# Query and key projections of one attention layer, from three 256-column products to one of 256 and one of 512 in two PSUM banks

## The chip, the cores and the metric

The kernel runs on one core of one Trainium2 chip. The metric is the device time of one execution in microseconds (us), and the figure that is compared is the median of several runs.

## The reference

An encoder of four layers on 256 tokens with 1024 features in float32. Each layer has a half-step SwiGLU block, a token mixer and a second half-step SwiGLU block, every one behind an RMSNorm and added to the residual. The mixer of the first layer, the one that the change touches, is attention in three groups (windows of 128, 512 and 2048 with dilations 1, 4 and 16), eight heads of 64 in each, mixed by a softmax over the groups' log-sum-exps:

```python
qkv = (u @ w_qkv).reshape(b, s, N_GROUPS_A, 3, HEADS_PER_GROUP, HEAD_DIM_A)
for g, (win, dil) in enumerate(DIL_PATTERNS):
    o, l = _dilated_group(qkv[:, :, g, 0], qkv[:, :, g, 1], qkv[:, :, g, 2], win, dil, ...)
wts = jax.nn.softmax(jnp.stack(lses, 0), axis=0)
o = jnp.einsum('gbsh,gbshd->bshd', wts, jnp.stack(outs, 0))
return o.reshape(b, s, ATTN_WIDTH).astype(u.dtype) @ w_o
```

## The kernel before

**High and low parts.** Every large product is made of float32 operands that are split into a high part (fp32r, rounded) and a low part (the rest): w = wh + wl, x = xh + xl, and w·x is taken as wh·xh + wh·xl + wl·xh. `mm3` issues these (through `mm`, L91; transposes are L94) as three matmuls of 256 columns into the same 256 columns of a PSUM bank. `wide`, which the SwiGLU blocks use, issues two: wl·xh with 256 columns, and wh with both parts of x side by side in 512 columns. The two halves of a bank then hold wl·xh + wh·xh and wh·xl, and are added when the bank is read.

**Weights.** They come in blocks of 128x2048. `dma_block` (L169) loads one on SP's queue into one of four `raw` buffers. `split_block` makes the high part on ScalarE (`w`, L178) and the low part on VectorE (`w`, L181) in one of four `w` buffers. `take` hands a block to the products in a fixed order, `done` counts one as used up, and `pump(n)` splits as many new blocks as were used up, n at most. All engines' instructions are issued in the order of the program; there is no scheduler.

**PSUM.** There are eight banks, four called A and four called B. In this stage `ab()` gives the B bank that was taken longest ago, and `dbank(j)` gives A bank j. Taking a bank waits for nothing by itself: its first matmul waits until the last readers of the bank's earlier contents are done.

**The attention stage (`mix0`).** `vproj` makes the values of the three groups. `proj(hp, g)` makes queries and keys of head pair hp in group g (hp from 0 to 3, g from 0 to 2): eight steps k over the 1024 input features, each of them for c = 0 (queries, 128 features) and c = 1 (keys). The eighth step reads the bank on VectorE, times the norm factors `Rqk` (L1068), into `qk`. The twelve projections are called p00 to p32 here, by hp and g.

The other pieces are `S(i)` for head pair i // 2 and query half i % 2 (scores of two heads: matmuls A<-qk, then `s` L1097 and the row maximum `m` L1100 on VectorE), `E(u)` (exponential, ScalarE, L1107), `N(u)` (division by the sum, VectorE, L1115), `T(u)` (four transposes on TensorE, L94, and a copy to `pt` on ScalarE, L1125) and `V(hp)` (products of `pt` and `vt`, into a bank of `ab()`, read by ScalarE and VectorE into `og`, L656 and L657). `S` and `T` use A banks for the first three head pairs, and banks of `ab()` for the last.

p00, p01 and p02 stand alone. Then, for hp = 0, 1, 2, the pieces of head pair hp are interleaved with the 24 steps of the projections of hp + 1:

```python
def part(i, a, b, c, pump=0, lead=0):
    u = 2 * i
    r = [(None, lead), (lambda: S(i), 0)]
    if i and i % 2 == 0:
        r.append((lambda: V(i // 2 - 1), 0))
    r += [(lambda f=f, n=n: f(u + n), 0) for f in (E, N) for n in range(2)]
    return r + [(lambda: self.pump(pump), a), (lambda: T(u), b), (lambda: T(u + 1), c)]
```

The number beside each piece says how many steps follow it: `lead` steps ahead of S, 6 after the pump, 2 after the first T, 4 (less the lead) after the second. For the last head pair there is no projection left. S(6) stands right behind p32, and its filler is the output projection (`A<-og,w`).

Of the kernel before, what the change touches and what calls it, by code (L numbers as in the profile page):

```python
# [11 lines left out]
AF = mybir.ActivationFunctionType  # L12
ALU = mybir.AluOpType
# [25 lines left out]
class Enc:  # L39
# [973 lines left out]
    def mix0(self):  # L1013
        nc = self.nc
# [32 lines left out]
        Rqk = self.sb(ev, [128, 512], F32, "Rqk")  # L1047
# [6 lines left out]
        def proj(hp, g):  # L1054

            def step(k, state={}):
                if k == 0:
                    state["w"] = self.take(("qk", hp, g))
                    state["p"] = self.ab()
                w, p = state["w"], state["p"]  # L1060
                for c in range(2):
                    sl = slice(128 * c, 128 * c + 128)
                    self.mm3(p[:, 256 * c:256 * c + 256], w[:, :, k, sl], self.xk(k),
                             start=k == 0 and c == 0, stop=k == 7)
                if k == 7:
                    self.done()
                    q = self.sb(ev, [128, 512], F32, f"qk{g}", 2)
                    nc.vector.tensor_tensor(q, p, Rqk, ALU.mult)  # L1068
                    qk[hp, g] = q
                    if hp == 0 and g < 2:  # L1070
                        self.pump()
            st = {}
            return [lambda k=k: step(k, st) for k in range(8)]
# [83 lines left out]
        def pfill(hp):  # L1157
            return [f for g in range(3) for f in proj(hp, g)]
# [8 lines that stand above are left out]
            return r + [(lambda: self.pump(pump), a), (lambda: T(u), b), (lambda: T(u + 1), c)]  # L1167

        for hp in range(3):
            lead = 2 if hp else 0  # L1170
            self.interleave(part(2 * hp, 6, 2, 4 - lead, 2, lead) + part(2 * hp + 1, 6, 2, 4, 1), pfill(hp + 1))

        r = [lambda f=f, u=u: f(u) for f, u in
# [492 lines left out]
```

## Time and profile before

| | |
|---|---|
| median of 3 runs | 1922.9 us (1922.87 to 1923.37) |
| profiled execution, its own time | 1922.22 us |
| its span, first to last instruction | 1920.4 us |
| TensorE busy | 1895.0 us (99%) |
| VectorE busy | 1401.6 us (73%) |
| ScalarE busy | 999.2 us (52%) |
| mean granted TensorE clock | 0.997 |

The span is the part of an execution that the trace covers, and 1.8 us of the execution's time lie around it. PE is TensorE's matmuls, PEld its weight loads, DVE VectorE, ACT ScalarE, SP the queue of the loads. Matmul ends are modelled, so the time of one matmul in a row is read from starts: the next start less this one.

### The profile page before, as it was taken

The page shows a single profiled execution, that of the slowest core. Times are in us where ns is not written, and L with a number is a line of the kernel's source. Part 1 is how long each engine was busy: PE and PEld are TensorE (multiplying, and loading weights), DVE is VectorE, ACT ScalarE, POOL GpSimd, SP SyncE. Part 2 cuts the span into 40 slices and gives each one's busy share as a digit, 9 for nine tenths or more (in the row PEclk, how much of TensorE's full clock was granted, in tenths as well). Part 3 has the DMA queues.
Part 4 walks back from the last instruction along what each step waited for, and adds up shares of the span by engine and source line. Part 5 has one row for each costly group of instructions (what it writes and reads, how often), then busy time and mean ns, then how long its engine had stood idle before and what let it go on. Part 6 is the DMA issues. An engine that isn't in the chain of part 4 may idle for free.

```text
span 1920.4 us, 28519 instructions
## 1 busy us (share of the span) xinstructions
PE 1895.0 (99%) x11936; PEld 1662.2 (87%) x11936; DVE 1401.6 (73%) x1877; ACT 999.2 (52%) x1272; POOL 10.7 (1%) x28
## 2 busy tenths in 40 slices
PE   8999999999999999999999999999999999999998
PEld 7888899888888898788888889988888888788887
DVE  7776667876687787887768776787777766678774
ACT  6554444655464544655446454555445546746543
POOL 0000000000000000000000000000000000000000
PEclk9999999999999999999999999999999999999999
DMA  7655533465555544256546554365546544435650
GB/s 266 222 195 192 192 132 132 154 219 190 183 187 194 194 162 147 89 179 216 179 172 208 187 184 168 132 219 192 181 162 223 203 162 159 154 111 183 212 184 36
DMA packets 48689, 338.63 MB, mean 176 GB/s; under 512 B 5488, under 2 KB 5664, under 8 KB 8240
## 3 DMA queue, kind: packets, MB, share of 16 engines
q1 hardware_dynamic: 47952, 335.11, 50.1%
q8 instruction: 93, 1.52, 0.3%
q0 software_dynamic: 608, 1.71, 0.3%
q14 instruction: 36, 0.29, 0.0%
HBM read 335.74 MB, written 1.05 MB: 175 GB/s over the span
## 4 chain that ended last, share of the span: by engine, by line
PE 90%; DVE 5%; ACT 2%; issue 1%; DMA 0%; SPq 0%; DVEq 0%; POOL 0%; POOLq 0%; ACTq 0%
PE B L91 47%; PE A L91 42%; DVE w L181 1%; ACT w L178 1%; DVE zc L787 1%; PE A L94 0%; DMA h<-in_x_dram 0%; DVE x L315 0%; ACT x L313 0%; DVE h L292 0%; DVE acc L366 0%; PE B L94 0%; DVE h L290 0%; SPq L225 0%; DVE s L1097 0%
## 5 line engine op out<-in xcount | busy, mean ns | idle before, releaser
L181 DVE TENSOR_TENSOR w<-raw,w 128x2048 fp32r<-128x2048 f32 x315 | 719.3, 2290 | 274.4 <-ACT w L178 274.3
L178 ACT ACTIVATE w<-raw 128x2048 fp32r<-128x2048 f32 x315 | 598.5, 1909 | 99.9 <-PE B L91 40.7
L91 PE MATMUL B<-x,w 128*128 128x256 f32 (+1 forms) x3968 | 641.5, 321 | 2.7 <-DVE w L181 1.5
L91 PEld LDWEIGHTS B<-x,w 128*128 128x128 f32 x3968 | 569.5, 189 | 69.8 <-issue 2.7
L91 PE MATMUL A<-x,w 128*128 128x256 f32 x3008 | 521.6, 335 | 9.7 <-DVE w L657 7.5
L91 PEld LDWEIGHTS A<-x,w 128*128 128x128 f32 x3008 | 455.6, 189 | 72.9 <-DVE w L657 7.5
L91 PE MATMUL B<-g,w 128*128 128x256 f32 (+1 forms) x1408 | 250.8, 336 | 0.0
L91 PE MATMUL A<-g,w 128*128 128x256 f32 (+1 forms) x1408 | 250.4, 336 | 0.0
L91 PEld LDWEIGHTS A<-g,w 128*128 128x128 f32 x1408 | 216.7, 187 | 31.4
L91 PEld LDWEIGHTS B<-g,w 128*128 128x128 f32 x1408 | 216.6, 187 | 31.4
L656 ACT ACTIVATE g<-br 128x512 fp32r<-128x512 f32 x88 | 55.6, 632 | 250.1 <-DVE br L497 250.1
L491 DVE TENSOR_TENSOR sl<-sl,R 128x512 f32<-128x512 f32 x176 | 120.3, 687 | 2.5
L657 DVE TENSOR_TENSOR g<-br,g 128x512 fp32r<-128x512 f32 x88 | 60.9, 692 | 61.5 <-ACT g L656 61.5
L313 ACT ACTIVATE x<-h,cols 128x256 fp32r<-128x256 f32 x88 | 39.9, 501 | 70.9 <-DVE h L290 51.2
L483 ACT ACTIVATE br<-A 128x256 f32<-128x256 f32 x88 | 30.4, 386 | 74.9 <-PE A L91 74.9
L483 ACT ACTIVATE br<-B 128x256 f32<-128x256 f32 x88 | 30.3, 385 | 74.8 <-PE B L91 74.8
L494 ACT ACTIVATE sl<-sl 128x512 f32<-128x512 f32 x88 | 55.0, 628 | 25.8 <-DVE sl L491 25.8
L497 DVE TENSOR_TENSOR br<-sl,br 128x512 f32<-128x512 f32 x88 | 60.4, 686 | 0.6
L483 ACT ACTIVATE sl<-A 128x256 f32<-128x256 f32 x88 | 30.1, 378 | 52.0 <-PE A L91 52.0
L483 ACT ACTIVATE sl<-B 128x256 f32<-128x256 f32 x88 | 29.8, 377 | 49.5 <-PE B L91 49.5
L91 PE MATMUL B<-w,x 128*128 128x512 f32 (+1 forms) x216 | 50.0, 379 | 0.0
L488 DVE TENSOR_TENSOR sl<-sl,A 128x256 f32<-128x256 f32 x88 | 33.1, 416 | 21.8 <-ACT sl L483 21.8
(290 smaller groups left out, 1085.6 us busy)
## 6 DMA issues: line engine op xcount, KB each, us to landing
raw<-in_ffn_w_dram SPq DMA_DIRECT2D x262, 1024.0 KB, 4.8
raw<-in_attn_w_qk_dram SPq DMA_DIRECT2D x12, 1024.0 KB, 4.8
raw<-in_conv_w_pw_dram SPq DMA_DIRECT2D x12, 1024.0 KB, 4.8
raw<-in_gla_w_vr_dram SPq DMA_DIRECT2D x8, 1024.0 KB, 5.5
raw<-in_attn_w_v_dram SPq DMA_DIRECT2D x6, 1024.0 KB, 4.7
raw<-in_fnet_w_dram SPq DMA_DIRECT2D x4, 1024.0 KB, 4.8
raw<-in_gla_w_in_dram SPq DMA_DIRECT2D x4, 1024.0 KB, 4.8
raw<-in_gla_w_o_dram SPq DMA_DIRECT2D x4, 1024.0 KB, 4.7
```

What stands on the lines that cost most here:

```text
L91: return self.nc.tensor.matmul(out, lhsT, rhs, start=start, stop=stop, skip_group_check=True)
L178: self.nc.scalar.activation(w[:, 0], raw, AF.Copy)
L181: (eng or self.nc.vector).tensor_tensor(w[:, 1], raw, f32(w[:, 0]), ALU.subtract)
L313: nc.scalar.activation(xh[:, c], h[:, c], AF.Copy, scale=g[c])
L483: nc.scalar.activation(t[:, c], P[c][:, 1], AF.Copy)
L488: nc.vector.tensor_tensor(t[:, c], t[:, c], P[c][:, 0], ALU.add)
L491: nc.vector.tensor_tensor(t, t, self.Rb(), ALU.mult)
L494: nc.scalar.activation(t, t, AF.Silu)
L497: nc.vector.tensor_tensor(br, sl, br, ALU.mult)
L656: self.nc.scalar.activation(p[:, 0], src, AF.Copy)
L657: self.nc.vector.tensor_tensor(p[:, 1], src, f32(p[:, 0]), ALU.subtract)
L787: nc.vector.scalar_tensor_tensor(o, x, w, o, ALU.mult, ALU.add)
```

## The change

In `proj` each step issues, for each c, the two matmuls of `wide` in place of the three of `mm3`, and queries and keys have a bank each, so a projection takes two banks of `ab()` where it took one. After the eighth step ScalarE copies the upper half of each bank to `q` (two copies), VectorE adds the lower half of each (two additions), and then multiplies by `Rqk`. For hp = 1 and 2 the lead is three steps where it was two, and the steps after the second T are one where they were two.

```diff
             def step(k, state={}):
                 if k == 0:
                     state["w"] = self.take(("qk", hp, g))
-                    state["p"] = self.ab()
+                    state["p"] = [self.v2(self.ab()) for _ in range(2)]
                 w, p = state["w"], state["p"]
                 for c in range(2):
-                    sl = slice(128 * c, 128 * c + 128)
-                    self.mm3(p[:, 256 * c:256 * c + 256], w[:, :, k, sl], self.xk(k),
-                             start=k == 0 and c == 0, stop=k == 7)
+                    self.wide(p, c, w[:, :, :, 128 * c:128 * c + 128], k, self.xk(k), k == 0, k == 7)
                 if k == 7:
                     self.done()
                     q = self.sb(ev, [128, 512], F32, f"qk{g}", 2)
-                    nc.vector.tensor_tensor(q, p, Rqk, ALU.mult)
+                    for c in range(2):
+                        nc.scalar.activation(q[:, 256 * c:256 * c + 256], p[c][:, 1], AF.Copy)
+                    for c in range(2):
+                        o = q[:, 256 * c:256 * c + 256]
+                        nc.vector.tensor_tensor(o, o, p[c][:, 0], ALU.add)
+                    nc.vector.tensor_tensor(q, q, Rqk, ALU.mult)
                     qk[hp, g] = q
...
         for hp in range(3):
-            lead = 2 if hp else 0
+            lead = 3 if hp else 0
             self.interleave(part(2 * hp, 6, 2, 4 - lead, 2, lead) + part(2 * hp + 1, 6, 2, 4, 1), pfill(hp + 1))
```

`wide`, which it now calls:

```python
def wide(self, p, c, w, k, x, start, stop):
    self.mm(p[c][:, 0], w[:, 1, k], x[:, 0], start, False)
    self.mm(p[c], w[:, 0, k], x, False, stop)
```

## Rows read from the trace of the kernel before

**Rows 1.** Page, part 1: busy time of each engine over the span.
```profile
PE 1895.0 (99%) x11936; PEld 1662.2 (87%) x11936; DVE 1401.6 (73%) x1877; ACT 999.2 (52%) x1272; POOL 10.7 (1%) x28
```

**Rows 2.** Busy time by stretch (engines, clock, DMA share, GB/s): projections, interleaved part, SwiGLU.
```profile
229.60:246.80 17.20, 17.20 (x145) 17.14 (x143) 8.26 (x5) 7.72 (x6) 0.00 (x0) 1.00 0.58 190
246.80:315.40 68.60, 68.60 (x602) 65.74 (x600) 49.21 (x91) 31.25 (x46) 0.00 (x0) 1.00 0.34 123
...
370.00:470.00 100.00, 100.00 (x577) 87.37 (x576) 74.49 (x80) 54.92 (x66) 0.00 (x0) 1.00 0.61 210
```

**Rows 3.** TensorE in order of time, attention stage: start, us, line, operands, count.
```profile
229.51 17.43 PE L91 MATMUL B<-x,w 128*128 128x256 f32 x144
246.88 1.35 PE L91 MATMUL A<-qk 64*128 64x256 f32 x12
248.15 4.58 PE L91 MATMUL B<-x,w 128*128 128x256 f32 x36
...
270.04 1.15 PE L91 MATMUL A<-qk 64*128 64x256 f32 x12
271.12 1.96 PE L91 MATMUL B<-pt,vt 128*64 128x256 f32 x24
273.01 4.58 PE L91 MATMUL B<-x,w 128*128 128x256 f32 x36
277.43 0.60 PE L94 MATMUL A<-ident,e 128*128 128x128 f32 x4
...
296.43 4.58 PE L91 MATMUL B<-x,w 128*128 128x256 f32 x36
...
315.44 2.23 PE L91 MATMUL B<-qk 64*128 64x256 f32 x24
317.78 1.96 PE L91 MATMUL B<-pt,vt 128*64 128x256 f32 x24
```

**Rows 4.** ScalarE in order of time, after S(2) and V(0).
```profile
275.02 3.70 ACT L178 ACTIVATE w<-raw 128x2048 fp32r<-128x2048 f32 x2
```

**Rows 5.** VectorE in order of time, p02, p11, p20 and p30 being read.
```profile
246.99 0.69 DVE L1068 TENSOR_TENSOR qk<-B,Rqk 128x512 f32<-128x512 f32 x1 [1.52 <-PE B L91]
...
266.90 0.68 DVE L1068 TENSOR_TENSOR qk<-B,Rqk 128x512 f32<-128x512 f32 x1
...
276.95 4.49 DVE L181 TENSOR_TENSOR w<-raw,w 128x2048 fp32r<-128x2048 f32 x2 [1.12 <-ACT w L178]
281.36 0.69 DVE L1068 TENSOR_TENSOR qk<-B,Rqk 128x512 f32<-128x512 f32 x1
...
304.78 0.68 DVE L1068 TENSOR_TENSOR qk<-B,Rqk 128x512 f32<-128x512 f32 x1
```

**Rows 6.** Order of time in a SwiGLU block: copies and additions of halves.
```profile
383.45 0.63 ACT L483 ACTIVATE sl<-B 128x256 f32<-128x256 f32 x2
...
386.19 0.74 DVE L488 TENSOR_TENSOR sl<-sl,B 128x256 f32<-128x256 f32 x2
```

**Rows 7.** What TensorE waited for, whole span: total us, times, longest.
```profile
PE A L91 <- DVE w L657: 7.5, 1, 7.5
PE B L91 <- DVE lr L406: 1.7, 1, 1.7
```

**Rows 8.** Busy time by stretch around a fall of the granted clock.
```profile
780.00:785.00 5.00, 3.87 (x32) 3.35 (x24) 4.40 (x9) 4.17 (x8) 0.00 (x0) 1.00 0.01 2
785.00:788.00 3.00, 1.29 (x6) 1.04 (x6) 2.63 (x9) 1.86 (x4) 0.00 (x0) 0.70 0.00 0
788.00:790.00 2.00, 0.85 (x4) 0.73 (x4) 0.59 (x3) 1.20 (x2) 0.00 (x0) 0.50 0.00 0
790.00:792.00 2.00, 2.00 (x12) 2.00 (x10) 0.70 (x3) 1.20 (x2) 0.00 (x0) 0.50 0.00 0
792.00:794.00 2.00, 2.00 (x14) 2.00 (x14) 1.70 (x5) 1.26 (x3) 0.00 (x0) 0.74 0.00 0
...
800.00:802.00 2.00, 2.00 (x19) 2.00 (x18) 2.00 (x2) 2.00 (x5) 0.00 (x0) 1.00 0.72 295
```

## Prediction

> **What bounds the kernel now.** I read the page's busy times first: TensorE is busy for 99% of the span, VectorE for 73%, ScalarE for 52% [rows 1]. That is an average over twelve stages, so the windows of the attention stage come next. While the first three projections run, and while the others are interleaved with scores and transposes, TensorE is busy without a gap, VectorE for 49.2 of 68.6 us and ScalarE for 31.3 [rows 2]. So here TensorE sets the end: each nanosecond that its own instructions lose or gain moves the end, and so does each wait that is put in front of it. The other engines' work is free as long as TensorE finds what it needs. So I looked for what TensorE will need under the change that it does not need now, and read the three engines in order of time around the two places where a projection ends just before other work depends on it.
>
> **Products.** Before, p00 to p02 run alone: 144 matmuls from 229.51 to 246.88 [rows 3], 17.37 us, 120.6 ns for each, so 724 ns for a step of six. The form after runs in the SwiGLU blocks: 577 matmuls in 100 us, half of 256 and half of 512 columns, with the same shapes of weights and x [rows 2], so 347 ns for a pair and 694 ns for a step of two pairs. The columns of a step are the same, 1536. If columns alone counted, the gain would be nothing, the lower bound. The weight loads tell the forms apart: in the projections PEld is busy for 17.14 of 17.20 us, in the SwiGLU stretch for 87.4 of 100 [rows 2], so the old form also stands at the pace of its loads, one of which the new form drops. I take the pitches as they are: 29.5 ns a step, 96 steps, **-2.8 us**.
>
> The Trainium skill (TensorE: Matmul & The Clock Gate, Back-to-back issue gap) puts an isolated matmul at its columns over 2.4 GHz and about 2.5 ns. By it 192 matmuls fewer would give 0.5 us, an estimate from that page; the rows show some 14 ns more than the columns for each matmul in both forms, and the measurement decides.
>
> **More reading of banks.** For each projection ScalarE gets two copies (0.63 us a pair) and VectorE two additions (0.74 us a pair) [rows 6]; the multiplication stays. Over twelve that is 7.6 and 8.9 us. VectorE has 19 us idle in the interleaved part alone, ScalarE 37 [rows 2], so neither becomes the bound by its sum. The order of their queues is another matter.
>
> **Scores right behind a projection.** S(0) follows p02 and S(6) follows p32 with nothing between. The first two groups of their products need older projections, the third needs the newest. Before, VectorE's multiplication starts 0.11 us after TensorE reaches S(0) and takes 0.69 [rows 3, 5]. S(0) takes 1.27 us, S(6) and S(7) together 2.34, where S(2), with steps ahead of it, takes 1.08 [rows 3], so the chain just shows. After, the chain is longer by the copies (0.63), the second addition (0.42, the first lies beside the second copy) and a hand-over of some 0.05: 1.1 us, all visible, since it showed already. Both engines are idle then. Two places: **+2.2 us**. The lower bound is 0, if other work lay between; none does. At S(2) and S(4) three steps (2.1 us) and the first two groups cover a chain of 1.9 us: nothing.
>
> **Banks.** This is the part that decides. `ab()` hands out the four B banks in a ring. Call the ring's places 0 to 3. A projection now takes two, V one. With hp = 0 there is no V, and the projections alternate between pairs: p10 has 0, 1; p11 has 2, 3; p12 has 0, 1. Then p20 takes 2, 3 at its first step, V(0) takes 0, and p21 gets 1 and 2. So p21's second bank, for its keys, is the one that holds p20's queries, and p20 has only just ended. p22 gets 3, 0; p30 gets 1, 2; V(1) gets 3; p31 gets 0 and 1, and 1 again holds the queries of the projection that has just ended. Twice, then, the third matmul of a projection (its first for c = 1) has to wait until VectorE has added the first half of the projection before. With one bank a projection, p20, V(0) and p21 had 0, 1 and 2, and nothing met.
>
> How late is that addition? p20's last step lies behind V(0), five steps on. The six steps after the pump are k = 3 to 7 of p20 and k = 0 of p21. TensorE leaves V(0) at 273.01 [rows 3]; five steps and one pair later, 3.47 + 0.35 = 3.82 us, it stands before the wait. But the pump ahead of these steps has put two blocks on ScalarE (275.02, 3.70 us) and VectorE (276.95, 4.49 us) [rows 4, 5]. In the trace p20's multiplication starts at 281.36, though TensorE had ended p20 by 277.43 [rows 3, 5]; no one was waiting for it. That is 8.35 us after V(0), and for p30 it is 304.78 - 296.43, again 8.35 [rows 3, 5]. That chain (scores, maximum, exponential, splits) does not hang on the steps, so it stays where it is relative to V. p20's copies queue behind the same splits on ScalarE, which end at 278.72 [rows 4], and are done well before. So the first addition takes the place of the multiplication: 8.35 + 0.42 + 0.05 = 8.82 us after V(0). The wait is 8.82 - 3.82 = 5.0 us. TensorE's matmuls stand in one queue, so T(4), T(5), the steps and S(3) all wait behind it, and no other engine catches this up. Two places: **+10.0 us**. The upper bound is a wait for all of p20's reading, the second addition and the multiplication too: 1.0 us more at each, 12. The lower bound is 0, if the additions could go ahead of the splits; the queue's order excludes it, unless I have the ring wrong. All other banks come free in time: the nearest is p20's, whose earlier content is p11. Its multiplication starts at 266.90 [rows 5], so two additions in that place end at 267.64; p12 ends two steps ahead of S(2) at 270.04 [rows 3], 268.59, less 0.35 for its twelve shorter steps: p20 starts 0.6 us after the additions.
>
> **The clock.** After the first 8 us the longest wait of TensorE in this trace is 1.7 us [rows 7]. Around it the granted clock fell to its lower level, 1.2 GHz: 0.70 in one stretch, 0.50 in two, 0.74 in the next [rows 8], which makes 1.8 + 4.0 + 1.0 = 6.8 us at that level. Before the fall TensorE had been busy for 3.87 of 5 us, then for 1.29 of 3, partly with thin products. A wait of 5.0 us inside dense work has no like in the trace. I take it that the clock falls at each. In the low stretch TensorE started 12 matmuls in 2 us against 19 at 2.4 GHz [rows 8], so each microsecond loses 0.37. Between no fall and 6.8 us of work at the lower level lie 0 and 2.5 us for each wait. Part of a low stretch passes during the wait, so I take half: **+2.6 us** for both, bounds 0 and 5.0.
>
> The Trainium skill (TensorE: Matmul & The Clock Gate, A second HAM failure mode: psum-queue depth-cycling) tells of a kernel that went in turn through PSUM banks and whose clock swung between both levels because TensorE idled between groups of matmuls. It speaks against this change; rows 8 agree that gaps can bring the clock down, but show no gap over a bank.
>
> **The sum.** -2.8 + 2.2 + 10.0 + 2.6 = +12.0 us against the profiled execution's own 1922.2 us: 1934.2. The median of the runs stands 0.7 us above that execution, so 1934.9, and I forecast **1935 us**.
>
> **Rivals.**
> 1. No wait for the banks, because I have the ring or the reader wrong: -2.8 + 2.2, 1922.3 us, no change. It decides if VectorE's first addition is done 3.8 us after V. For it speaks that a bank is waited for only where readers overlap; against it stands that the multiplication at 281.36 is late by far more than a step.
> 2. One of the two places stays free, say because a piece falls on another place of the ring: 1922.9 - 0.6 + 5.0 + 1.3 = 1928.6 us. The equal 8.35 us at both speak against it.
> 3. VectorE also comes too late for S(2) and S(4). Its slack there is about 1.0 us. A block split 2.29 us long in its way would cost 1.3 us at each, 1937.5 us. In the trace VectorE waits for TensorE ahead of p02 [rows 5], and nothing is pumped between p11 and S(2), which speaks against it.
>
> **How the numbers follow.** Both waits as worked out, with or without the clock: 0.84. Rival 1: 0.08, rival 2: 0.04, rival 3: 0.04. The forecast is the first. Its bounds, from the median: without the clock 1922.9 + 9.4 = 1932.3; with 12 us of waits and 5.0 of clock 1939.3. No gain from the products would add 2.8. The range is **1929 to 1939 us**: from about rival 2 to the upper bound, with rival 1 and some of the rest left out. A measurement of this kernel can tell 0.2% from no change, 3.8 us, so slower is anything over 1926.7. Slower gets all but rival 1 and a little: 0.90. Rival 1 gives 0.08 to no change, and 0.02 to faster, should the scores' chain be hidden too.
>
> **What would show it.** In the changed kernel's order of time TensorE stands still for about 5 us twice, one pair into p21 and into p31, released by an addition of VectorE into `qk` that starts right behind two splits. The granted clock is low for some microseconds behind each. S(0) takes about 2.4 us, S(6) with S(7) about 3.4. Steps in the projections take 694 ns. I am wrong if TensorE runs through p21 without a gap, if the gap is much shorter because VectorE gets to the addition before the splits, or if the clock stays at its full level throughout.

## The result, and the profile after

The changed kernel takes 1935.74 us (median of 4 runs, 1935.08 to 1936.74) against 1922.88 us for the kernel before (4 runs, 1920.91 to 1923.37), a ratio of 1.0071 with a 95% interval from 1.0059 to 1.0082: 12.9 us slower, outside the 0.2% that tell a change from none. The forecast was 1935 us in 1929 to 1939. The profiled execution took 1936.74 us, the slowest of its four; its span is 1935.0 us.

The page's first part after the change, beside [rows 1]: 192 matmuls fewer, 24 instructions more each on VectorE and ScalarE. TensorE is busy for 3.8 us more, with fewer matmuls, and idle for 36.2 us of the span where it was 25.4; where that lies, the page does not say.

```profile
PE 1898.8 (98%) x11744; PEld 1655.3 (86%) x11744; DVE 1411.1 (73%) x1901; ACT 1007.1 (52%) x1296; POOL 10.7 (1%) x28
```

What TensorE waited for in the attention stage (total us, times, longest). Before, the only such wait from 200 to 340 us was one of 0.2 us. L1070 is the addition of the halves, L1071 the multiplication by `Rqk`.

```profile
PE B L91 <- DVE qk L1070: 9.4, 2, 4.7
PE A L91 <- DVE qk L1071: 0.8, 1, 0.8
PE B L91 <- DVE qk L1071: 0.8, 1, 0.8
PE B L94 <- DVE e L1118: 0.3, 1, 0.3
```

TensorE in order of time, which answers to [rows 3]:

```profile
230.26 17.11 PE L91 MATMUL B<-x,w 128*128 128x256 f32 x96
247.30 0.92 PE L91 MATMUL A<-qk 64*128 64x256 f32 x8
249.03 0.49 PE L91 MATMUL A<-qk 64*128 64x128 f32 x4 [0.80 <-DVE qk L1071]
249.45 4.45 PE L91 MATMUL B<-x,w 128*128 128x256 f32 x24
...
272.60 1.96 PE L91 MATMUL B<-pt,vt 128*64 128x256 f32 x24
274.49 4.15 PE L91 MATMUL B<-x,w 128*128 128x256 f32 x22
283.31 1.01 PE L91 MATMUL B<-x,w 128*128 128x256 f32 x2 [4.68 <-DVE qk L1070]
...
288.98 1.15 PE L91 MATMUL A<-qk 64*128 64x256 f32 x12
...
302.69 1.96 PE L91 MATMUL B<-pt,vt 128*64 128x256 f32 x24
304.58 4.15 PE L91 MATMUL B<-x,w 128*128 128x256 f32 x22
313.41 1.01 PE L91 MATMUL B<-x,w 128*128 128x256 f32 x2 [4.68 <-DVE qk L1070]
...
319.36 1.15 PE L91 MATMUL A<-qk 64*128 64x256 f32 x12
...
329.85 0.92 PE L91 MATMUL B<-qk 64*128 64x256 f32 x8
331.57 1.37 PE L91 MATMUL B<-qk 64*128 64x128 f32 x16 [0.80 <-DVE qk L1071]
332.97 1.96 PE L91 MATMUL B<-pt,vt 128*64 128x256 f32 x24
```

The 22 matmuls behind V(0) are k = 3 to 7 of p20 and the pair for c = 0 of p21. The first matmul for c = 1 starts 8.82 us after V(0) has ended (283.31 - 274.49), and 8.83 after V(1).

VectorE around the end of p02 and of p20 and p30, beside [rows 5]:

```profile
247.48 0.77 DVE L1070 TENSOR_TENSOR qk<-qk,B 128x256 f32<-128x256 f32 x2 [1.20 <-ACT qk L1067]
248.28 0.69 DVE L1071 TENSOR_TENSOR qk<-qk,Rqk 128x512 f32<-128x512 f32 x1
...
278.43 4.49 DVE L181 TENSOR_TENSOR w<-raw,w 128x2048 fp32r<-128x2048 f32 x2 [1.13 <-ACT w L178]
282.85 0.74 DVE L1070 TENSOR_TENSOR qk<-qk,B 128x256 f32<-128x256 f32 x2
...
312.94 0.75 DVE L1070 TENSOR_TENSOR qk<-qk,B 128x256 f32<-128x256 f32 x2
```

The additions start where the two subtractions end. 282.85 and 0.42 for the first make 283.27, and TensorE starts at 283.31. ScalarE is no part of it: p20's copies start at 280.10.

The granted clock (the figure behind POOL's) around the two waits, in windows, beside [rows 8]:

```profile
281.00:284.00 3.00, 0.69 (x2) 0.63 (x3) 2.97 (x4) 0.00 (x0) 0.00 (x0) 0.52 0.72 240
284.00:288.00 4.00, 4.00 (x16) 3.41 (x15) 0.31 (x1) 0.60 (x1) 0.00 (x0) 0.51 0.88 340
288.00:292.00 4.00, 4.00 (x30) 3.32 (x29) 1.81 (x6) 0.81 (x2) 0.00 (x0) 1.00 0.01 4
...
312.00:314.00 2.00, 0.59 (x2) 0.59 (x3) 1.97 (x4) 0.00 (x0) 0.00 (x0) 0.50 0.82 311
314.00:318.00 4.00, 4.00 (x15) 3.35 (x15) 0.41 (x1) 0.60 (x1) 0.00 (x0) 0.50 0.84 352
318.00:320.00 2.00, 2.00 (x14) 1.67 (x14) 0.00 (x0) 0.60 (x1) 0.00 (x0) 0.83 0.00 0
```

The clock falls to 1.2 GHz while TensorE stands still. By these windows it is low for 6.8 us at each place, and 4.6 and 5.3 us of that lie behind the wait: 15 or 16 matmuls start in 4 us, then 30.

### The profile page after: what moved, and what is told of

It reads as the page before. It is cut to its first block, busy times and chain, and to the rows that moved or that the text cites. A ratio compares the mean times of both kernels' runs of the same rounds, so it can differ in the third digit from the quotient of the medians.

```text
span 1935.0 us, 28186 instructions
## 1 busy us (share of the span) xinstructions
PE 1898.8 (98%) x11744; PEld 1655.3 (86%) x11744; DVE 1411.1 (73%) x1901; ACT 1007.1 (52%) x1296; POOL 10.7 (1%) x28
## 4 chain that ended last, share of the span: by engine, by line
PE 88%; DVE 6%; ACT 3%; issue 2%; DMA 1%; SPq 0%; DVEq 0%; POOL 0%; POOLq 0%; ACTq 0%
PE B L91 46%; PE A L91 41%; DVE w L181 2%; ACT w L178 1%; DVE zc L787 1%; PE A L94 0%; DMA h<-in_x_dram 0%; ACT x L313 0%; DVE x L315 0%; DVE s L1100 0%; DVE h L290 0%; DVE m L1103 0%; DVE h L292 0%; DMA craw<-in_c_tri_dram 0%; DVE acc L366 0%
## 5 line engine op out<-in xcount | busy, mean ns | idle before, releaser
L91 PE MATMUL B<-x,w 128*128 128x256 f32 x3776 | 643.5, 330 | 11.0 <-DVE qk L1070 9.4
L91 PEld LDWEIGHTS B<-x,w 128*128 128x128 f32 x3776 | 560.5, 189 | 86.3 <-DVE qk L1070 10.0
```

Source lines behind the costliest of these rows:

```text
L91: return self.nc.tensor.matmul(out, lhsT, rhs, start=start, stop=stop, skip_group_check=True)
```

## The experiments

The whole kernel's time varies by some microseconds from run to run, so the stage itself is measured too: from p00's first matmul to the first of V(3), read from TensorE's rows in order of time. Beside the experiments the kernel before ran at medians of 1922.28 and 1922.25 us.

| kernel | median us | p00 | V(3) | stage us |
|---|---|---|---|---|
| before | 1922.88 | 229.51 | 329.55 | 100.04 |
| changed | 1935.74 | 230.26 | 344.80 | 114.54 |
| V in an A bank | 1921.95 | 229.66 | 331.39 | 101.73 |
| the wait filled with products | 1932.60 | 229.87 | 339.92 | 110.05 |
| old products, two banks | 1935.90 | 230.12 | 342.33 | 112.21 |
| two splits on GpSimd | 1928.89 | 229.85 | 336.80 | 106.95 |
| lead of two | 1932.09 | 230.13 | 341.76 | 111.63 |
| V in an A bank, old form at p02, p32 | 1924.88 | 229.85 | 330.00 | 100.15 |
| the same, lead of two | 1923.52 | 230.09 | 328.95 | 98.86 |

**V out of the ring.**

```diff
-            p = self.ab()
+            p = self.ab() if hp > 1 else self.dbank(2)
             pt = [pts.pop((hp, hh)) for hh in range(2)]
```

> The changed kernel, but V(0) and V(1) write to A bank 2 instead of a bank of the ring, so that projections always alternate between two pairs of B banks and none needs a bank of the one just ended. Theory (the two waits for banks, 4.7 us each, and the lower clock behind them, about 2.4 us each, make the loss): TensorE runs through p21 and p31 without a gap, the clock stays at its full level in the stage, and the time is 1935.7 - 9.4 - 4.8 = 1921.5 us, level with the kernel before within 2 us. Rival (the extra copies and additions load ScalarE and VectorE, and TensorE would wait for them at other places anyway): above 1930 us, with waits of several us elsewhere in the stage.

Measured: 1921.95 us (10 runs), a ratio to before of 1.0001 (0.9991 to 1.0010). One line of bank choice takes the loss back, with all the copies, additions and products left in. The granted clock stays at 1.00 in the stage:

```profile
230.00:331.00 101.00, 98.03 (x676) 83.76 (x675) 78.74 (x148) 54.72 (x90) 0.00 (x0) 1.00 0.35 125
```

The waits that remain from 200 to 360 us:

```profile
PE B L91 <- DVE w L181: 1.0, 1, 1.0
PE A L94 <- DVE e L1118: 1.0, 2, 0.5
PE B L91 <- DVE qk L1071: 0.9, 1, 0.9
PE A L91 <- DVE qk L1071: 0.8, 1, 0.8
PE B L94 <- DVE e L1118: 0.3, 1, 0.3
```

The rival falls: no wait of several us appears. The first of these rows lies behind the stage and is there before, too. But two new waits of 0.5 us stand in front of T(6) and T(10): VectorE now adds and multiplies p20 and p30 between the splits and the scores of S(3) and S(5). TensorE's rows give the path from V(0) to S(3) without a wait for a bank, 281.29 - 272.00 = 9.29 us, where the changed kernel takes 288.98 - 272.60 = 16.38.

```profile
272.00 1.96 PE L91 MATMUL A<-pt,vt 128*64 128x256 f32 x24
...
281.29 1.15 PE L91 MATMUL A<-qk 64*128 64x256 f32 x12
```

**The wait filled with products.** It computes all that the changed kernel does, and 72 products that nothing reads.

```diff
                     self.wide(p, c, w[:, :, :, 128 * c:128 * c + 128], k, self.xk(k), k == 0, k == 7)
+                    if hp > 1 and (g, k, c) == (1, 0, 0):
+                        for _ in range(36):
+                            self.mm(self.dbank(3)[:, 0:256], w[:, 0, k, 0:128], self.xk(k)[:, 0], True, True)
```

> The changed kernel with 36 extra products of 256 columns (p21 and p31, first step, into a free A bank, never read) put between the products for c = 0 and c = 1, where TensorE waits. They take 36 x 0.12 = 4.3 us, less than the wait of 4.7, so the release by VectorE's addition comes at the same time as without them. Theory (part of the loss is the clock, which falls because TensorE stands still): no fall of the clock in the stage, and p21 to S(3) goes at full speed: 1935.7 - 4.8 = 1930.9 us, though more is computed. Rival (the wait alone is the loss, and the low clock costs nothing that was not waited for anyway): 1935.7 us or more.

Measured: 1932.60 us, 3.1 us less than the changed kernel; the stage is 4.5 us shorter. TensorE in order of time:

```profile
272.20 1.96 PE L91 MATMUL B<-pt,vt 128*64 128x256 f32 x24
274.08 4.15 PE L91 MATMUL B<-x,w 128*128 128x256 f32 x22
278.07 4.48 PE L91 MATMUL A<-x,w 128*128 128x256 f32 x36
282.91 0.62 PE L91 MATMUL B<-x,w 128*128 128x256 f32 x2 [0.37 <-DVE qk L1073]
...
286.44 1.15 PE L91 MATMUL A<-qk 64*128 64x256 f32 x12
```

The release comes at the same place, 8.83 us after V(0), and from there to S(3) it takes 3.53 us, where the changed kernel takes 288.98 - 283.31 = 5.67; at the second place it is 3.51 against 319.36 - 313.41 = 5.95. The granted clock is 1.00 from 270 to 325 us. More work in less time: the low clock alone costs 2.1 and 2.4 us in the profiled execution. The medians show 3.1 us for both together. The changed kernel's trace is that of the slowest of its runs; that the fall was shorter in the others would explain the difference, but no trace shows it. From V(0) to S(3) it is 14.24 us here against 9.29 with no wait for a bank, so the wait by itself costs 4.95 us, and 14.23 - 9.30 = 4.93 at the second place.

**Old products, two banks.**

```diff
-                    self.wide(p, c, w[:, :, :, 128 * c:128 * c + 128], k, self.xk(k), k == 0, k == 7)
+                    self.mm3(p[c][:, 0], w[:, :, k, 128 * c:128 * c + 128], self.xk(k), k == 0, k == 7)
...
                     for c in range(2):
-                        nc.scalar.activation(q[:, 256 * c:256 * c + 256], p[c][:, 1], AF.Copy)
-                    for c in range(2):
-                        o = q[:, 256 * c:256 * c + 256]
-                        nc.vector.tensor_tensor(o, o, p[c][:, 0], ALU.add)
-                    nc.vector.tensor_tensor(q, q, Rqk, ALU.mult)
+                        s = slice(256 * c, 256 * c + 256)
+                        nc.vector.tensor_tensor(q[:, s], p[c][:, 0], Rqk[:, s], ALU.mult)
```

> The three products of the kernel before, but a bank for each 128 features as in the changed kernel, and VectorE's multiplication in two halves straight from the banks: no copies, no additions, no products of 512 columns. Theory (the ring of banks makes the loss, whatever the products): TensorE arrives at the wait 3.96 us after V and is released at 8.8 by the first half of the multiplication, so two waits of about 4.6 us with a lower clock behind each, and no gain from products nor loss at S(0) and S(6): 1922.9 + 9.2 + 4.8 = 1936.9 us. Rival (the longer reading makes the loss): 1923 us, no waits over 1 us.

Measured: 1935.90 us, ratio to before 1.0068 (1.0053 to 1.0083). The second bank makes a loss of the same size without the new products, the copies and the additions. The lead of three steps stands in this run as in the changed kernel. TensorE's row at p21:

```profile
282.94 1.01 PE L91 MATMUL B<-x,w 128*128 128x256 f32 x3 [4.60 <-DVE qk L1068]
```

At p31 the wait is 4.61 us. S(0) takes no longer than before. In the profiled execution the clock was low for 3.4 us at each place, half as long as in the changed kernel's (granted 0.51 from 282.5 to 286, then 1.00), and the stage is 2.3 us shorter than there.

**Two splits' low parts on GpSimd.**

```diff
-            return r + [(lambda: self.pump(pump), a), (lambda: T(u), b), (lambda: T(u + 1), c)]
+            return r + [(lambda: self.pump(pump, eng=nc.gpsimd if i in (2, 4) else None), a), (lambda: T(u), b), (lambda: T(u + 1), c)]
```

> The changed kernel with the low parts of the two blocks that are split ahead of the end of p20 and of p30 computed on GpSimd instead of VectorE. Theory (the first addition is late because it stands behind two subtractions of 2.29 us in VectorE's queue, and behind two conversions in ScalarE's): the addition is now held only by ScalarE, whose copies start 5.6 us after V, so the release moves from 8.8 to about 6.5 us after V and each wait from 4.7 to about 2.3 us. 1935.7 - 4.7 = 1931.0 us if the clock still falls at both, 1926.2 us if at neither. Rival (the wait ends with something else than VectorE's queue): waits of 4.7 us as before. GpSimd's time for a block of 128x2048 stands in no row, so it can bring a wait for weights at p22 or p30.

Measured: 1928.89 us, 6.9 us less than the changed kernel, between the two numbers. All engines in order of time at p20's end:

```profile
278.06 9.55 POOL L181 TENSOR_TENSOR w<-raw,w 128x2048 fp32r<-128x2048 f32 x2 [275.81 <-ACT w L178]
279.68 0.63 ACT L1067 ACTIVATE qk<-B 128x256 f32<-128x256 f32 x2
280.07 0.75 DVE L1070 TENSOR_TENSOR qk<-qk,B 128x256 f32<-128x256 f32 x2 [3.18 <-ACT qk L1067]
280.55 0.30 PEld L91 LDWEIGHTS B<-x,w 128*128 128x128 f32 x2 [2.66 <-DVE qk L1070]
280.55 0.62 PE L91 MATMUL B<-x,w 128*128 128x256 f32 x2 [2.34 <-DVE qk L1070]
280.86 2.30 DVE L1071 TENSOR_TENSOR qk<-qk,Rqk 128x512 f32<-128x512 f32 x1
```

With VectorE's queue empty, the addition waits for ScalarE's copies, which stand behind two conversions; the wait is 2.34 us at both places. So VectorE's queue made half of it. No wait for weights came. After the first wait S(3) follows 3.54 us later, at full clock; after the second the clock was low and S(5) took 5.07.

**The lead back to two.**

```diff
-            lead = 3 if hp else 0
+            lead = 2 if hp else 0
```

> The changed kernel with the lead back at two steps for hp = 1 and 2; all else as changed. The ring of banks is the same, so both waits stay. Theory: S(2) and S(4), and with them the chain of VectorE that ends the wait, come one step (0.70 us) earlier, and T(4) and T(8) (0.35 us) lie ahead of the wait and no longer behind it, so each place costs 1.05 us less, with waits of about 3.6 us in place of 4.7: 1935.7 - 2.1 = 1933.6 us, if the clock falls as before. Rival (the longer lead is what S(2) and S(4) need under the longer reading): waits of 0.3 us or more appear at S(2) and S(4), and the time stays at 1935.7 us or more.

Measured: 1932.09 us, 3.6 us less than the changed kernel, and 2.9 by the stages, more than the 2.1 expected. The waits are 3.54 us each, and no wait appears at S(2) or S(4). Behind the first wait the granted clock was low only from 282.0 to 285.4 us, half as long as in the changed kernel, behind the second from 309.3 to 316.1; that can account for the rest. The third step of the lead, with this ring, puts T(4) and T(8) behind the wait and hides nothing.

**What is left, put together.** V in an A bank, and the old form for p02 and p32; then also a lead of two.

```diff
+                old = (hp, g) in ((0, 2), (3, 2))
...
+                if old:
+                    for c in range(2):
+                        self.mm3(p[:, 256 * c:256 * c + 256], w[:, :, k, 128 * c:128 * c + 128], self.xk(k),
+                                 start=k == 0 and c == 0, stop=k == 7)
```

> V(0) and V(1) in A bank 2 as in the run that did so alone (1921.95 us), and p02 and p32, which have S(0) and S(6) right behind them, in the old form: three products, one bank, one multiplication from the bank. Theory (the longer chain shows at S(0) and S(6) only): the waits of 0.80 and 0.89 us there fall back to about 0.1 each, 1.5 us less, while 16 steps lose 0.016 us each, 0.3 us more: 1921.95 - 1.2 = 1920.7 us. Rival (the chain is hidden by what follows S(0) and S(6) anyway): 1922 us.

> As the run before it, with the lead back at two steps. Theory (with the waits for banks gone, T(6) and T(10) wait 0.48 us each for VectorE, which now has p20's and p30's additions between the splits and the scores of S(3) and S(5); a step more between S(2) and S(3) gives VectorE 0.7 us more): both waits vanish, and none appears at S(2) and S(4), where two steps and two groups of scores, about 2.0 us, just cover the chain of 1.95: 1.0 us less than the run before it, 1919.7 us. Rival (two steps are too few at S(2) and S(4) under the longer reading): waits there of 0.3 us or more, and no gain over the run before it.

Measured: 1924.88 us (11 runs, 1920.13 to 1929.42) and 1923.52 us (11 runs, 1919.75 to 1928.10), ratios to before 1.0012 (1.0003 to 1.0021) and 1.0007 (0.9998 to 1.0016). The stage did what was expected, and a little more: 101.73 us with V in an A bank alone, then 100.15 and 98.86 us, and the second has only the old small wait of 0.2 us at T(12) left, beside 1.0 us behind the stage. The whole did not follow: 1920.7 and 1919.7 us were expected. So both were profiled once more.

> The same kernel as the one with V in an A bank and p02 and p32 in the old form, profiled once more, because its runs lay between 1920.1 and 1929.4 us while the profiled one was the fastest. Theory (the spread comes from other stages, where the granted clock falls in some executions and not in others): the attention stage, p00 to V(3), takes 100.2 us again within 0.3, whatever the time of the whole. Rival (the spread is in this stage): the stage is longer by what the whole is.

> The same with the lead of two steps, profiled once more, for the same question. Theory: the stage takes 98.9 us again within 0.3. Rival: it is longer by what the whole is.

Measured: 1922.29 and 1927.06 us, with stages of 329.97 - 229.82 = 100.15 and 328.84 - 230.00 = 98.84 us. The spread lies elsewhere. In the second one these windows, in the last mixer 1,270 us later, hold the time; the granted clock is 1.00 in all three in the kernel before:

```profile
1595.00:1600.00 5.00, 3.28 (x15) 2.55 (x15) 5.00 (x14) 3.15 (x7) 0.00 (x0) 0.78 0.95 356
1600.00:1605.00 5.00, 5.00 (x26) 5.00 (x25) 2.85 (x2) 1.50 (x1) 0.31 (x1) 0.50 0.13 26
1605.00:1610.00 5.00, 5.00 (x31) 5.00 (x32) 1.95 (x12) 0.00 (x0) 0.00 (x0) 0.69 0.51 198
```

Before, 44 and 45 matmuls start in the last two windows, here 26 and 31. TensorE has short waits there (1.3, 0.4 and 0.2 us), and the clock fell. In the first profiled execution of the same kernel it fell there too, but for a shorter time (0.50 from 1597 to 1600 us). From the last mixer's first `B<-x,w` product to its first `A<-la,lst` it is 47.4 us here (1591.75 to 1639.17), 44.0 in that other execution and 41.9 in the kernel before. The clock is only a part of the spread, though. The two profiled executions of the version with a lead of three differ by 2.2 us with the same stage; 1.0 of it lies in this same stretch (40.2 and 41.2 us), at a granted clock of 1.00 in both. And that version's six runs from 1924.1 to 1925.1 us have mean clocks of 0.996 and 0.997, where its fastest three have 0.997; none of the six was profiled, and what makes them longer is open. A stage that is 1.2 us shorter is not to be seen through that. The runs give no reason to call either version faster than the kernel before; the interval of the first even lies just above 1, by less than the 0.2%.

## Why the prediction was right

**Products.** Forecast -2.8 us; the size was off. p00 to p02 take 17.04 us for 24 steps in place of 17.37: 14 ns a step, not 29.5, which would be 1.3 us over 96 steps. In the interleaved part a step gains more: p10's first six take 4.29 us (249.45 to 253.74) where they took 4.42 (248.15 to 252.57), 22 ns each. What the other terms leave of the stage's 14.5 us gives 1.7 for all 96. The new form is slower in the first projections (710 ns a step) than in the SwiGLU blocks (694). Why is open; the pace of the weight loads, by which the forecast told the forms apart, does not set it there, since PEld is busy for only 14.45 of 16.80 us. The measured gain lies between the 0.5 us, an estimate, that the forecast took from the Trainium skill (TensorE: Matmul & The Clock Gate, Back-to-back issue gap) and the rows' pitch.

**Scores behind a projection.** Forecast +2.2; S(0) takes 249.45 - 247.30 = 2.15 us in place of 1.27, S(6) with S(7) 3.12 in place of 2.34: +1.7. The chain is shorter than worked out because queries have a bank of their own: ScalarE's first copy of p02 starts at 247.06, before TensorE has left the projection. That the wait is this chain is shown by the old form at these two places, which took 1.6 us off the stage.

**Banks.** Forecast two waits of 5.0 us, released 8.82 us after V; measured 8.82 and 8.83, at a cost of 4.95 and 4.93. Shown from three sides: another bank for V removes both, two banks with the old products bring them back, and emptier queues move the release as worked out. The forecast's detail that VectorE's queue and not ScalarE's holds the addition holds too. With VectorE's queue emptied ScalarE's holds it, and TensorE is released 6.49 us after V.

**Clock.** Forecast +2.6 with bounds 0 and 5.0; 4.6 in the profiled execution, 3.1 between medians. It fell at both waits, as forecast. The length of the low stretch, 6.8 us, came out as taken from [rows 8]; its price was too small on two counts. Not half of it lay behind the wait but 4.6 and 5.3 us, because the clock fell only 2.2 and 1.6 us before the wait's end. And each microsecond of it lost 0.46 us of work (2.1 of 4.6, 2.4 of 5.3), not the 0.37 of [rows 8]. With a wait of 4.7 us for a bank the clock fell, with the wait filled or gone it did not. The Trainium skill (TensorE: Matmul & The Clock Gate, A second HAM failure mode: psum-queue depth-cycling) tells of a kernel that paused often and briefly between groups of matmuls as it went through PSUM banks, and whose clock swung; this case agrees that idling over banks can bring the clock down, but its waits are two single ones of 4.7 us.

**The sum.** 9.9 + 4.6 + 1.7 - 1.7 = 14.5 us in the profiled execution's stage, against +12.0; the sum closes because the products' 1.7 is what the others leave. Products gave 1.1 us less than forecast and the clock cost 2.0 more, while the scores cost 0.5 less. Between medians the change costs 12.9 us. The mechanism and its largest term came as forecast, but that the median lies within 1 us of 1935 is in part luck: the one execution that was taken apart is 2.5 us above its sum. Of the rivals none came: no place stayed free, S(2) and S(4) do not wait.

## What to carry to other kernels

Before a tile takes two buffers of a ring in place of one, write down who holds each buffer at each taking, pieces that break the pairing included. Where a new holder follows right behind the old one, the wait is what stands ahead of the reader in its in-order queue, and the trace of before shows it already as a late instruction that nobody waited for. A wait that empties TensorE for several microseconds is to be priced with the slower clock behind it. And a gain of one microsecond in a stage is to be measured in the stage, not in the whole.

## What the runs showed that was not expected

GpSimd took 4.5 to 5.0 us for a low part of 128x2048 that takes VectorE 2.29, and while it ran VectorE's multiplication of 128x512 took 2.30 us in place of 0.69. A wait of 2.34 us brought the clock down at one of two like places and not at the other. How long the lower level lasted differed as well: 3.4 us behind the first wait and 6.8 at the second with a lead of two, and at one place in the last mixer 3.4 and 10.2 us in two executions of one kernel. So part of what a wait costs can be a matter of the run.
